# Attention scores of 64-deep heads as row-tiled groups of four matmuls, with new priority keys for the scheduler

## The chip, the cores and the metric

One Trainium2 chip, eight cores, two dies of four cores (0 to 3 and 4 to 7). Every core runs the same program on two of the sixteen sequences; no core talks to another. The metric is device time of the slowest core in microseconds (us); lower is better. Runs come in a fast state and a slow one (in the slow one a die, or both, shows a lower granted TensorE clock, down to 0.81 as the mean of a whole run); 12 of the 13 kernels run here had slow runs. All comparisons below are between fast runs or, where it is said, between cores of an undisturbed die.

## The reference, cut to what matters

A decoder layer: RMSNorm, one projection into a convolution part and an attention part, output projection, SwiGLU feed-forward (2816 wide), a gated per-layer embedding, final RMSNorm. The change is in the attention: 8 heads, each only 64 deep, sequence 4096, causal, with a decay per position.

```python
# logit[t, s] = q_t.k_s / sqrt(64) + c[t] - c[s],  c[t] = sum_{j<=t} log f[j]
s = jnp.einsum('bqhd,bkhd->bhqk', q_blk, kf)        # contraction over d = 64
s = s + c_q[..., :, None] - c_k[:, :, None, :]
s = jnp.where(k_pos[None, :] <= q_pos[:, None], s, -jnp.inf)
out = softmax(s) @ v
```

## The kernel before

The program is a list of operations, each with a priority key and a guessed duration; a list scheduler written in Python sets the order of each engine's queue when the kernel is built. The order is then fixed. 512 queries are one block; work of three blocks is mixed (attention of block n+1, feed-forward of block n, projections of block n+2), so that TensorE always has something to do. The keys say which of it goes first.

```python
KT = sb("KT", [128, 4, S], BF16)        # two heads stacked: head 2p in rows 0-63, head 2p+1 in 64-127
QT = sb("QT", [128, 8, T], BF16)        # per head; the other head's 64 rows are zero
qS = Pool("S", banks[0:3])              # 8 PSUM banks: scores,
qO = Pool("O", banks[3:5])              # attention output,
qD = Pool("Dn", banks[5:8])             # everything else
# ... [cut]
def fqk(e, st=st, hp=hp, kt=kt, c0=c0, dg=dg, h=h):          # one key tile of 128 keys
    ins = e.matmul(st.ap()[:, c0:T], lhsT=KT[:, hp, kt * 128:(kt + 1) * 128], rhs=QT[:, h, c0:T],
                   start=True, stop=not dg)
    if dg:                                                    # diagonal tile: decay, causal mask
        e.matmul(st.ap()[:, c0:T], lhsT=sel[:, h * 128:(h + 1) * 128], rhs=crow[:, c0:T],
                 start=False, stop=False)
        ins = e.matmul(st.ap()[:, c0:c0 + 128], lhsT=identb[:], rhs=maskb[:], start=False, stop=True)
    return ins
# ... then on ScalarE: P = exp(scores + bK); LOOK = 3 units later on TensorE: O += VA . P
```

Each score matmul contracts over 128 rows though a head has 64: the other 64 rows multiply zeros.

The softmax here doesn't subtract the row's maximum and nothing guards it: scores larger than these inputs give would overflow.

Of the kernel before, what the change touches and what calls it, by code (L numbers as in the profile page):

```python
# [7 lines left out]
F32 = mybir.dt.float32  # L8
# [11 lines left out]
SEQ_PER_CORE = 2  # L20
NEG = -30000.0
PAIRED = False

# [369 lines left out]
def build(nc, nblk=8, nseq=SEQ_PER_CORE):  # L393
# [22 lines left out]
    ones_d = dram("ones", [128, 128])  # L416
    maskb_d = dram("maskb", [128, 128])
    bdiag_d = dram("bdiag", [128, 128])
# [12 lines left out]
    onesf = sb("onesf", [128, 128], F32)  # L431
    maskb = sb("maskb_s", [128, 128], BF16)
    bdiag = sb("bdiag_s", [128, 128], BF16)
# [30 lines left out]
    B["sel"] = cdma("pool", sel[:], sel_d[:, :], 8 * K64, key=-1.19)  # L464
    B["maskb"] = cdma("pool", maskb[:], maskb_d[:, :], K64, key=-1.19)
    B["cw"] = cdma("sp", cw[:], cw_d[:, :], 8192, key=-1.0)
# [10 lines left out]

    KT = sb("KT", [128, 4, S], BF16)
    VA = sb("VA", [128, 32, 8, 65], BF16)
# [3 lines left out]
    ccar = sb("ccar", [128, 4, 2], F32)  # L483
    BKT = [[Buf() for _ in range(8)] for _ in range(4)]
    BVA = [Buf() for _ in range(32)]
# [28 lines left out]
    stat = sb("stat", [128, 64], F32)  # L514
    fst = sb("fst", [128, 8, 32], F32)
    Bfst = Buf()
# [5 lines left out]
    pXB = pool("xnbf", 2, [128, D], BF16)  # L522
    pP = pool("P", 5, [128, T], BF16)
    pCS = pool("cs", 1, [128, T], F32)
# [8 lines left out]
    banks = [es.enter_context(nc.psum_tensor(f"ps{i}", [128, 512], F32)) for i in range(8)]  # L533
    qS = Pool("S", banks[0:3])
    qO = Pool("O", banks[3:5])
    qD = Pool("Dn", banks[5:8])

    P.op("pool", lambda e: e.memset(VA[:, :, :, 64:65], 1.0), 1.0, -8.0, writes=BVA)
    P.op("pool", lambda e: e.memset(QT[:], 0.0), 2.0, -8.0, writes=BQT)
    P.op("pool", lambda e: e.memset(crow[:], 0.0), 0.6, -8.0, writes=[Bcrow])  # L540
# [121 lines left out]
    def qkv(m, kn, kk, kv, kq):  # L662
# [15 lines left out]
        for hp in range(4):  # L678
            t = Tile(qD)
            mm_group(t, fm_mats(wk[hp // 2], (hp % 2) * 128, w), kk + e_ * hp, xr + [wk[hp // 2]], gate=[BKT[hp][blk]])  # L680
            P.op("dve", lambda e, t=t, hp=hp: e.tensor_copy(out=KT[:, hp, q0:q0 + T], in_=t.ap()[:]),
                 0.69, kk + e_ * hp, reads=[t], writes=[BKT[hp][blk]])
        wv = [wload(g, kv) for g in plan["v"]]
# [33 lines left out]
        for hp in range(4):  # L717
            t = Tile(qD)
            mm_group(t, fm_mats(wq[hp // 2], (hp % 2) * 128, w), kq + e_ * hp, xr + [wq[hp // 2]], gate=[BQT[2 * hp], BQT[2 * hp + 1]])
            P.op("act", lambda e, t=t, hp=hp: e.activation(out=QT[0:64, 2 * hp, :], in_=t.ap()[0:64, :],  # L720
                                                           func=AF.Copy, scale=0.125),
                 0.6, kq + e_ * hp - 0.1, reads=[t], writes=[BQT[2 * hp]])
            P.op("dve", lambda e, t=t, hp=hp: e.tensor_scalar(out=QT[64:128, 2 * hp + 1, :], in0=t.ap()[64:128, :],
                                                              scalar1=0.125, scalar2=None, op0=ALU.mult),
                 0.69, kq + e_ * hp - 0.1, reads=[t], writes=[BQT[2 * hp + 1]])

# [54 lines left out]
    def decay(m, key):  # L781

        sq, blk = divmod(m, nblk)
        rel = fst[:, 6, :]
        P.op("dve", lambda e: e.tensor_copy(out=bK[:, 4 * blk:4 * blk + 4, :], in_=rel.rearrange("p (a b) -> p a b", a=4)),
             0.12, key, reads=[Brel], writes=[BbK])
        if blk:
            cb = carry[:, blk % 2, :].unsqueeze(1).to_broadcast([128, 4 * blk, 8])
            P.op("dve", lambda e: e.tensor_tensor(out=bK[:, 0:4 * blk, :], in0=cK[:, 0:4 * blk, :], in1=cb,
                                                  op=ALU.subtract),  # L790
                 0.35, key, reads=BcK[0:blk] + [Bcarry[blk % 2]], writes=[BbK])
        bx = Tile(qD)

        def ftr(e):
            ins = None
            for tt in range(4):
                ins = e.transpose(out=bx.ap()[0:8, tt * 128:(tt + 1) * 128], in_=fst[:, 6, 8 * tt:8 * tt + 8],
                                  identity=identf[:])
            return ins
        P.op("pe", ftr, 0.45, key, reads=[Brel, B["identf"]], writes=[bx], after=busy([Bcrow]))  # L800
        P.op("act", lambda e: e.activation(out=crow[0:8, :], in_=bx.ap()[0:8, :], func=AF.Copy, scale=-1.0),
             0.6, key - 0.1, reads=[bx], writes=[Bcrow])


    def attention(m, k0, k1):
        sq, blk = divmod(m, nblk)
        decay(m, k0 - 0.02)
        LOOK = 3
        units = []
# [30 lines left out]
        def post(h, o, key):  # L840
            q_ = osq[h % 2]
            P.op("act", lambda e: e.activation(out=q_[0:65, :], in_=o.ap()[0:65, :], func=AF.Square),
                 0.6, key - 0.1, reads=[o], writes=[Bosq[h % 2]])
            mt = Tile(qD)
            P.op("pe", lambda e: e.matmul(mt.ap()[:], lhsT=wn[:, :], rhs=q_[:, :], start=True, stop=True), MM,  # L845
                 key - 0.1, reads=[Bosq[h % 2], B["wn"]], writes=[mt])
            y0 = rsqrt_big(mt, 64, key - 0.1)
            if h % 2 == 0:
                dst = yTa[0:64, h // 2, :]
            else:  # L850
                dst = yTa[64:128, h // 2, :]
            P.op("dve", lambda e: e.scalar_tensor_tensor(out=dst, in0=o.ap()[0:64, :], scalar=gattn[:, h:h + 1],  # L852
                                                         in1=y0.ap()[0:64, :], op0=ALU.mult, op1=ALU.mult),
                 0.75, key - 0.1, reads=[o, y0, B["gattn"]], writes=[ByTa[h]])

        for i in range(N + LOOK):
            if i < N:
                h, kt, c0, dg, ui, nu = units[i]
                hp = h // 2
                if ui == 0 and blk:  # L860
# [7 lines left out]
                    P.op("act", lambda e, bt=bt, et=et: e.activation(out=et.ap()[0:65, :], in_=bt.ap()[0:65, :],  # L868
                                                                     func=AF.Exp), 0.6, K(i),
                         reads=[bt], writes=[et])  # L870
                st = Tile(qS)
                pt = Tile(pP)

                def fqk(e, st=st, hp=hp, kt=kt, c0=c0, dg=dg, h=h):
                    ins = e.matmul(st.ap()[:, c0:T], lhsT=KT[:, hp, kt * 128:(kt + 1) * 128], rhs=QT[:, h, c0:T],  # L875
                                   start=True, stop=not dg)
                    if dg:
                        e.matmul(st.ap()[:, c0:T], lhsT=sel[:, h * 128:(h + 1) * 128], rhs=crow[:, c0:T],  # L878
                                 start=False, stop=False)
                        ins = e.matmul(st.ap()[:, c0:c0 + 128], lhsT=identb[:], rhs=maskb[:], start=False, stop=True)  # L880
                    return ins
                w = (T - c0) / T
                rd = [BKT[hp][kt // 4], BQT[h]]
                if dg:
                    rd += [Bcrow, B["sel"], B["identb"], B["maskb"]]
                last_qk = P.op("pe", fqk, MM * w * (2 if dg else 1) + (0.06 if dg else 0.0), K(i), reads=rd,
                               writes=[st], after=[last_qk])
                P.op("act", lambda e, st=st, pt=pt, c0=c0, kt=kt, h=h: e.activation(  # L888
                    out=pt.ap()[:, c0:T], in_=st.ap()[:, c0:T], func=AF.Exp, bias=bK[:, kt, h:h + 1], scale=1.0),
                    0.17 + (T - c0) / 1200.0, K(i), reads=[st, BbK], writes=[pt])  # L890
                pend.append((h, kt, c0, dg, ui, nu, pt))
            if i >= LOOK:
# [219 lines left out]
    for n in range(-2, NB):  # L1112
# [7 lines left out]
        if 0 <= n + 1 < NB:  # L1120
# [3 lines left out]
            else:  # L1124
                conv(n + 1, b + 0.08, b + 0.5)
                attention(n + 1, b + 0.075, b + 0.95)
        if n >= 0:
            for tt in range(4):
                norm_tile((lambda tt=tt: hT[tt][:]), Bh[tt], tt, 1, 8, 4 + tt, b + 0.05)
            ffn(n, b + 0.07, b + 0.68)  # L1130
            for tt in range(4):
# [3 lines left out]
        if n + 2 < NB:  # L1135
# [4 lines left out]
            else:  # L1140
                qkv(n + 2, b + 0.5, b + 0.685, b + 0.8, b + 1.055)

# [9 lines left out]
def _host_consts():  # L1152
# [4 lines left out]
    c["ones"] = np.ones((128, 128), np.float32)  # L1157
    c["maskb"] = np.where(j[:, None] <= j[None, :], 0.0, NEG).astype(np.float32)
    c["bdiag"] = ((j[:, None] // 64) == (j[None, :] // 64)).astype(np.float32) / 64.0
# [5 lines left out]
    for h in range(8):  # L1165
        sel[h, h, :] = 1.0
    c["sel"] = sel.reshape(128, 1024)
    orow = np.zeros((128, 128), np.float32)
# [46 lines left out]
```

## Time and profile before

| what | value | read it as |
|---|---|---|
| time, fast runs | 4452.6 to 4455.2 us (6 of 16 runs) | the base of all that follows |
| time, slow runs | up to 5197 us | not compared |
| TensorE busy | 4310.9 us, 97% | the bound, but a modelled busy time: a 512-column matmul counts 380 ns on average, while starts are 216 ns apart (median) |
| TensorE waits that the profile lists | 123 us | 69 us of it in the first 150 and the last 200 us |
| ScalarE, VectorE, GpSimd busy | 51%, 59%, 4% | room |

TensorE waits for less than 3% of the time. Only less TensorE work, or work done two at a time, can help.

### The profile page before, as it was taken

Reading aid. Unit: us, or ns where it says so; the run is one execution under the profiler, and the core shown is the slowest. Engines: PE = TensorE matmul, PEld = TensorE weight load, DVE = VectorE, ACT = ScalarE, POOL = GpSimd, SP = SyncE. Lnnn points to the kernel's source line nnn. Section 1 sums busy time; section 2 is a strip of 40 time slices with the busy share of each in tenths; the row PEclk is TensorE's granted clock in tenths of the full one; section 3 lists DMA queues with packets and bytes.
Section 4 is the critical chain, followed back from the end, with each engine's and each line's share of the span. In section 5 each row is a group of like instructions: output and inputs, shape, how many; then the busy total and the mean of one; then the engine's idle time right before and its main releaser. Section 6 shows DMA issues by size and latency. Waiting matters only on the chain.

```text
span 4452.3 us, 75023 instructions; the slowest of 8 cores (4442.7 to 4452.3 us)
## 1 busy us (share of the span) xinstructions
PE 4310.9 (97%) x23984; PEld 2223.0 (50%) x23984; DVE 2644.5 (59%) x5380; ACT 2272.0 (51%) x4209; POOL 181.3 (4%) x405
## 2 busy tenths in 40 slices
PE   6899999999999999999999999999999999999987
PEld 3445454544545545445454545545454454554534
DVE  6667575665755645545676766757566464554444
ACT  3333354555646657567233444546455565666731
POOL 2110000000000000000000000000000000000000
PEclk9899999999999999999999999999999999999998
DMA  8796344343432433323444444434334343242232
GB/s 194 176 225 205 126 152 136 108 164 113 136 121 96 156 100 124 112 90 126 138 150 149 130 162 131 161 115 151 124 116 144 100 137 115 91 134 97 84 117 99
DMA packets 172924, 590.40 MB, mean 133 GB/s; under 512 B 19840, under 2 KB 28416, under 8 KB 172544
## 3 DMA queue, kind: packets, MB, share of 16 engines
q1 hardware_dynamic: 127952, 453.80, 30.8%
q0 software_dynamic: 44592, 131.79, 11.5%
q8 instruction: 207, 3.39, 0.3%
q14 instruction: 173, 1.42, 0.1%
HBM read 556.87 MB, written 61.87 MB: 139 GB/s over the span
## 4 chain that ended last, share of the span: by engine, by line
PE 91%; DVE 3%; issue 2%; DMA 2%; ACT 1%; POOL 0%; DVEq 0%; ACTq 0%; POOLq 0%; SPq 0%
PE ps L591 57%; PE ps L875 10%; PE ps L833 10%; PE ps L1079 5%; PE ps L709 2%; PE ps L639 2%; PE ps L878 1%; DMA xs<-x 1%; DVE ac L947 1%; DMA wslot<-wscr 1%; PE ps L1074 1%; PE ps L880 1%; PE ps L845 1%; PE ps L864 0%; DVE cu L937 0%
## 5 line engine op out<-in xcount | busy, mean ns | idle before, releaser
L888 ACT ACTIVATE P<-ps,bK 128x512 bf16<-128x512 f32 (+3 forms) x2304 | 1368.7, 650 | 811.8 <-PE ps L875 475.4
L591 PE MATMUL ps<-xnTd,wslot 128*128 128x512 bf16 x5792 | 1327.7, 380 | 9.2 <-DVE xnTd L644 3.4
L591 PEld LDWEIGHTS ps<-xnTd,wslot 128*128 128x128 bf16 x5792 | 562.0, 98 | 677.6 <-issue 33.6
L875 PE MATMUL ps<-QT,KT 128*128 128x512 bf16 (+3 forms) x2304 | 821.6, 362 | 13.5 <-ACT P L888 9.6
L833 PE MATMUL ps<-P,VA 128*65 128x512 bf16 (+3 forms) x2304 | 820.2, 363 | 5.6 <-DVE yTa L852 4.3
L591 PE MATMUL ps<-wslot,actT 128*128 128x512 bf16 x2816 | 652.5, 379 | 0.4 <-DVE h L976 0.4
L591 PE MATMUL ps<-xnTq,wslot 128*128 128x512 bf16 x2400 | 570.6, 382 | 13.3 <-DMA wslot<-wscr 7.8
L1021 DVE SCALAR_TENSOR_TENSOR tb<-th,ps 128x512 bf16<-128x512 f32 x352 | 241.2, 685 | 474.6 <-ACT th L1018 470.7
L1018 ACT ACTIVATE th<-ps 128x512 f32<-128x512 f32 x352 | 210.0, 596 | 484.5 <-PE ps L591 482.7
L591 PEld LDWEIGHTS ps<-wslot,actT 128*128 128x128 bf16 x2816 | 274.1, 98 | 318.6 <-issue 1.1
L976 DVE SCALAR_TENSOR_TENSOR h<-ps,h 128x512 f32<-128x512 f32 x256 | 176.2, 690 | 390.0 <-PE ps L591 388.2
L591 PEld LDWEIGHTS ps<-xnTq,wslot 128*128 128x128 bf16 x2400 | 231.2, 98 | 283.4 <-issue 33.7
L833 PEld LDWEIGHTS ps<-P,VA 128*65 128x65 bf16 x2304 | 257.1, 112 | 204.6 <-issue 11.8
L875 PEld LDWEIGHTS ps<-QT,KT 128*128 128x128 bf16 x2304 | 225.2, 98 | 261.8 <-issue 76.5
L622 ACT ACTIVATE xnbf<-h 128x1024 bf16<-128x1024 f32 x196 | 206.3, 1054 | 195.0 <-PE ps L639 76.7
L1025 DVE TENSOR_TENSOR actT<-tb,ps 128x512 bf16<-128x512 bf16 x352 | 241.1, 685 | 100.6 <-PE ps L591 96.7
L1079 PE MATMUL ps<-wslot,xnTd 128*128 128x256 bf16 x2048 | 247.9, 275 | 0.0
L1079 PEld LDWEIGHTS ps<-wslot,xnTd 128*128 128x128 bf16 x2048 | 201.8, 99 | 48.9 <-issue 1.0
L902 DVE TENSOR_TENSOR rs<-rs,ps 64x512 f32<-64x512 f32 (+1 forms) x192 | 130.1, 678 | 81.0 <-ACT rs L900 79.6
L644 DVE TENSOR_TENSOR xnTd<-ps,gpc_s 128x1024 bf16<-128x1024 bf16 x132 | 158.6, 1220 | 29.0 <-PE ps L639 27.1
L639 PE MATMUL ps<-identb,xnbf 128*128 128x128 bf16 x1536 | 119.2, 226 | 50.7 <-DVE stat L604 19.3
L1087 ACT ACTIVATE th<-ps 128x512 f32<-128x512 f32 x128 | 76.1, 594 | 166.7 <-PE ps L1079 132.4
(125 smaller groups left out, 4107.4 us busy)
## 6 DMA issues: line engine op xcount, KB each, us to landing
wslot<-wscr SPq DMA_DIRECT2D x795, 512.0 KB, 3.9
h<-x POOLq DMA_DIRECT2D x64, 512.0 KB, 6.3
y<-h POOLq DMA_DIRECT2D x64, 512.0 KB, 6.8
xs<-x POOLq DMA_DIRECT2D x60, 512.0 KB, 5.0
wslot<-wpack POOLq DMA_DIRECT2D x53, 512.0 KB, 14.7
wscr<-wslot SPq DMA_DIRECT2D x53, 512.0 KB, 10.9
wslot<-wscr SPq DMA_DIRECT2D x30, 256.0 KB, 2.7
pbf<-p POOLq DMA_DIRECT2D x16, 256.0 KB, 4.5
```

The costliest lines, as they stand in the source:

```text
L591: ins = e.matmul(out, lhsT=l, rhs=r, start=(i0 + i == 0), stop=(i0 + i == n - 1))
L622: P.op("act", lambda e: e.activation(out=xb.ap()[:], in_=src(), func=AF.Square, accum_out=stat[:, col:col + 1]), 1.25, key - 0.1, reads=[B ...
L639: ins = e.transpose(out=pv[:, kc * 128:(kc + 1) * 128], in_=xb.ap()[:, kc * 128:(kc + 1) * 128], identity=identb[:])
L644: P.op("dve", lambda e, pt=pt: e.tensor_tensor(out=xnT[which][:, :, tt * 128:(tt + 1) * 128], in0=pt.ap()[:].bitcast(BF16).rearrange("p (k ...
L833: P.op("pe", lambda e, o=o, kt=kt, h=h, pt=pt, c0=c0, first=first, last=last, ui=ui, dg=dg: e.matmul(o.ap()[0:65, c0:T], lhsT=VA[:, kt, h, ...
L875: ins = e.matmul(st.ap()[:, c0:T], lhsT=KT[:, hp, kt * 128:(kt + 1) * 128], rhs=QT[:, h, c0:T], start=True, stop=not dg)
L888: P.op("act", lambda e, st=st, pt=pt, c0=c0, kt=kt, h=h: e.activation(out=pt.ap()[:, c0:T], in_=st.ap()[:, c0:T], func=AF.Exp, bias=bK[:, ...
L976: P.op("dve", lambda e: e.scalar_tensor_tensor(out=hs, in0=t.ap()[:], scalar=scale, in1=hs, op0=ALU.mult, op1=ALU.add), 0.72, key - 0.05, ...
L1018: P.op("act", lambda e, tg=tg, th=th: e.activation(out=th.ap()[:], in_=tg.ap()[:], func=AF.Tanh, scale=0.5), 0.6, k - 0.1, reads=[tg], wri ...
L1021: P.op("dve", lambda e, tg=tg, th=th, tb=tb: e.scalar_tensor_tensor(out=tb.ap()[:], in0=th.ap()[:], scalar=1.0, in1=tg.ap()[:], op0=ALU.ad ...
L1025: P.op("dve", lambda e, tu=tu, tb=tb, j=j: e.tensor_tensor(out=actT[:, j, :], in0=tb.ap()[:], in1=tu.ap()[:], op=ALU.mult), 0.69, k - 0.1, ...
L1079: ins = e.matmul(tg.ap()[:, i * 256:(i + 1) * 256], lhsT=xnT[1][:, kc, ts], rhs=w8(wg[i])[:, kc, 0:256], start=False, stop=(kc == 7 and i ...
```

## The change

Intent: let matmuls of 64 rows run two at a time. Even key tiles of a head go to rows 0-63, odd ones to 64-127, the query of the head is copied to both halves, and four key tiles form a quad of four 64-row matmuls in alternating halves. The causal mask leaves TensorE: GpSimd zeroes the upper triangle of P. To find a fourth bank for scores, the other four are shared. Query and key evictions are split over ScalarE and VectorE. The keys of the scheduler are new.

```diff
-    KT = sb("KT", [128, 4, S], BF16)
+    KT = sb("KT", [128, 8, S // 2], BF16)
-    pP = pool("P", 5, [128, T], BF16)
+    pP = pool("P", 6, [128, T], BF16)
-    qS = Pool("S", banks[0:3])
-    qO = Pool("O", banks[3:5])
-    qD = Pool("Dn", banks[5:8])
+    qS = Pool("S", banks[0:4])
+    qO = Pool("Dn", banks[4:8])
+    qD = qO
 ... [cut: key and query evictions in four pieces, crow copied to rows 64-71, yTa product in two steps]
-        LOOK = 3
+        LOOK = 5
+                if ui % 4 == 0:
+                    quad = [Tile(qS) for _ in range(4)]
+                    def fqk(e, quad=quad, kt=kt, dg=dg, h=h):
+                        for dec in ((False, True) if dg else (False,)):
+                            for i in range(4):
+                                r = slice(64 * (i % 2), 64 * (i % 2) + 64)
+                                k_ = ((kt + i) // 2) * 128
+                                cc = 128 * i if dg else 0
+                                ins = e.matmul(quad[i].ap()[:, cc:T],
+                                               lhsT=sel[r, h * 128:(h + 1) * 128] if dec else KT[r, h, k_:k_ + 128],
+                                               rhs=crow[r, cc:T] if dec else QT[r, h, cc:T],
+                                               start=not dec, stop=dec or not dg)
+                        return ins
 ... [cut]
+                if dg:
+                    P.op("pool", lambda e, pt=pt, c0=c0: e.affine_select(
+                        out=pt.ap()[:, c0:c0 + 128], in_=pt.ap()[:, c0:c0 + 128], pattern=[[1, 128]],
+                        compare_op=ALU.is_ge, fill=zero_reg(e), base=0, channel_multiplier=-1),
+                        0.35, K(i), writes=[pt])
 ... [cut]
-                conv(n + 1, b + 0.08, b + 0.5)
-                attention(n + 1, b + 0.075, b + 0.95)
+                conv(n + 1, b + 0.08, b + 0.556)
+                attention(n + 1, b + 0.05, b + 0.815)
-            ffn(n, b + 0.07, b + 0.68)
+            ffn(n, b + 0.138, b + 0.695)
-                qkv(n + 2, b + 0.5, b + 0.685, b + 0.8, b + 1.055)
+                qkv(n + 2, b + 0.504, b + 0.685, b + 0.788, b + 1.017)
```

More of the change, by code (lines that the diff above doesn't have):

```diff
@@ L20 @@
 SEQ_PER_CORE = 2
-NEG = -30000.0
-PAIRED = False
 SEED_SCALE = -0.5 * float(np.log(2.0)) / 2.0 ** 23
@@ L416, in build @@
     ones_d = dram("ones", [128, 128])
-    maskb_d = dram("maskb", [128, 128])
     bdiag_d = dram("bdiag", [128, 128])
@@ L431, in build @@
     onesf = sb("onesf", [128, 128], F32)
-    maskb = sb("maskb_s", [128, 128], BF16)
     bdiag = sb("bdiag_s", [128, 128], BF16)
@@ L464, in build @@
     B["sel"] = cdma("pool", sel[:], sel_d[:, :], 8 * K64, key=-1.19)
-    B["maskb"] = cdma("pool", maskb[:], maskb_d[:, :], K64, key=-1.19)
     B["cw"] = cdma("sp", cw[:], cw_d[:, :], 8192, key=-1.0)
@@ L483, in build @@
     ccar = sb("ccar", [128, 4, 2], F32)
-    BKT = [[Buf() for _ in range(8)] for _ in range(4)]
+    BKT = [[Buf() for _ in range(8)] for _ in range(8)]
     BVA = [Buf() for _ in range(32)]
@@ L514, in build @@
     stat = sb("stat", [128, 64], F32)
-    fst = sb("fst", [128, 8, 32], F32)
+    fst = sb("fst", [128, 7, 32], F32)
     Bfst = Buf()
@@ L533, in build @@
     banks = [es.enter_context(nc.psum_tensor(f"ps{i}", [128, 512], F32)) for i in range(8)]
-    qS = Pool("S", banks[0:3])
-    qO = Pool("O", banks[3:5])
-    qD = Pool("Dn", banks[5:8])
+    qS = Pool("S", banks[0:4])
+    qO = Pool("Dn", banks[4:8])
+    qD = qO
     P.op("pool", lambda e: e.memset(VA[:, :, :, 64:65], 1.0), 1.0, -8.0, writes=BVA)
-    P.op("pool", lambda e: e.memset(QT[:], 0.0), 2.0, -8.0, writes=BQT)
     P.op("pool", lambda e: e.memset(crow[:], 0.0), 0.6, -8.0, writes=[Bcrow])
@@ L679, in qkv @@
             t = Tile(qD)
-            mm_group(t, fm_mats(wk[hp // 2], (hp % 2) * 128, w), kk + e_ * hp, xr + [wk[hp // 2]], gate=[BKT[hp][blk]])
-            P.op("dve", lambda e, t=t, hp=hp: e.tensor_copy(out=KT[:, hp, q0:q0 + T], in_=t.ap()[:]),
-                 0.69, kk + e_ * hp, reads=[t], writes=[BKT[hp][blk]])
+            mm_group(t, fm_mats(wk[hp // 2], (hp % 2) * 128, w), kk + e_ * hp, xr + [wk[hp // 2]], gate=[BKT[2 * hp][blk], BKT[2 * hp + 1][blk]])
+            for i in range(2):
+                for par in range(2):
+                    src = (lambda t=t, i=i, par=par: t.ap()[64 * i:64 * i + 64, :].rearrange(
+                        "p (a b c) -> p a b c", a=2, b=2)[:, :, par, :])
+                    dst = KT[64 * par:64 * par + 64, 2 * hp + i, q0 // 2:q0 // 2 + 256].rearrange("p (a c) -> p a c", a=2)
+                    if i == 0:
+                        P.op("act", lambda e, src=src, dst=dst: e.activation(out=dst, in_=src(), func=AF.Copy),
+                             0.39, kk + e_ * hp - 0.1, reads=[t], writes=[BKT[2 * hp + i][blk]])
+                    else:
+                        P.op("dve", lambda e, src=src, dst=dst: e.tensor_copy(out=dst, in_=src()),
+                             0.42, kk + e_ * hp - 0.1, reads=[t], writes=[BKT[2 * hp + i][blk]])
         wv = [wload(g, kv) for g in plan["v"]]
@@ L719, in qkv @@
             mm_group(t, fm_mats(wq[hp // 2], (hp % 2) * 128, w), kq + e_ * hp, xr + [wq[hp // 2]], gate=[BQT[2 * hp], BQT[2 * hp + 1]])
-            P.op("act", lambda e, t=t, hp=hp: e.activation(out=QT[0:64, 2 * hp, :], in_=t.ap()[0:64, :],
-                                                           func=AF.Copy, scale=0.125),
-                 0.6, kq + e_ * hp - 0.1, reads=[t], writes=[BQT[2 * hp]])
-            P.op("dve", lambda e, t=t, hp=hp: e.tensor_scalar(out=QT[64:128, 2 * hp + 1, :], in0=t.ap()[64:128, :],
-                                                              scalar1=0.125, scalar2=None, op0=ALU.mult),
-                 0.69, kq + e_ * hp - 0.1, reads=[t], writes=[BQT[2 * hp + 1]])
+            for i in range(2):
+                for half in range(2):
+                    src = (lambda t=t, i=i: t.ap()[64 * i:64 * i + 64, :])
+                    dst = QT[64 * half:64 * half + 64, 2 * hp + i, :]
+                    if i == 0:
+                        P.op("act", lambda e, src=src, dst=dst: e.activation(out=dst, in_=src(), func=AF.Copy, scale=0.125),
+                             0.6, kq + e_ * hp - 0.1, reads=[t], writes=[BQT[2 * hp + i]])
+                    else:
+                        P.op("dve", lambda e, src=src, dst=dst: e.tensor_scalar(
+                            out=dst, in0=src(), scalar1=0.125, scalar2=None, op0=ALU.mult),
+                            0.69, kq + e_ * hp - 0.1, reads=[t], writes=[BQT[2 * hp + i]])
     def gate_post(m, zt, key):
@@ L800, in decay, with zero_reg @@
         P.op("pe", ftr, 0.45, key, reads=[Brel, B["identf"]], writes=[bx], after=busy([Bcrow]))
-        P.op("act", lambda e: e.activation(out=crow[0:8, :], in_=bx.ap()[0:8, :], func=AF.Copy, scale=-1.0),
-             0.6, key - 0.1, reads=[bx], writes=[Bcrow])
+        for r in (0, 64):
+            P.op("act", lambda e, r=r: e.activation(out=crow[r:r + 8, :], in_=bx.ap()[0:8, :], func=AF.Copy, scale=-1.0),
+                 0.6, key - 0.1, reads=[bx], writes=[Bcrow])
+    zreg = []
+    def zero_reg(e):
+        if not zreg:
+            zreg.append(e.to_reg(0.0))
+        return zreg[0]
     def attention(m, k0, k1):
@@ L843, in post @@
                  0.6, key - 0.1, reads=[o], writes=[Bosq[h % 2]])
+            dst = yTa[0:64, h // 2, :] if h % 2 == 0 else yTa[64:128, h // 2, :]
+            P.op("dve", lambda e: e.tensor_scalar(out=dst, in0=o.ap()[0:64, :], scalar1=gattn[:, h:h + 1], scalar2=None,
+                                                  op0=ALU.mult), 0.69, key - 0.1, reads=[o, Bosq[h % 2], B["gattn"]], writes=[ByTa[h]])
             mt = Tile(qD)
@@ L851, in post @@
                 dst = yTa[64:128, h // 2, :]
-            P.op("dve", lambda e: e.scalar_tensor_tensor(out=dst, in0=o.ap()[0:64, :], scalar=gattn[:, h:h + 1],
-                                                         in1=y0.ap()[0:64, :], op0=ALU.mult, op1=ALU.mult),
-                 0.75, key - 0.1, reads=[o, y0, B["gattn"]], writes=[ByTa[h]])
+            P.op("dve", lambda e: e.tensor_tensor(out=dst, in0=dst, in1=y0.ap()[0:64, :], op=ALU.mult),
+                 0.69, key - 0.1, reads=[y0], writes=[ByTa[h]])
         for i in range(N + LOOK):
@@ L868, in attention @@
                     P.op("act", lambda e, bt=bt, et=et: e.activation(out=et.ap()[0:65, :], in_=bt.ap()[0:65, :],
-                                                                     func=AF.Exp), 0.6, K(i),
+                                                                     func=AF.Exp, scale=0.5), 0.6, K(i),
                          reads=[bt], writes=[et])
-                st = Tile(qS)
                 pt = Tile(pP)
-                def fqk(e, st=st, hp=hp, kt=kt, c0=c0, dg=dg, h=h):
-                    ins = e.matmul(st.ap()[:, c0:T], lhsT=KT[:, hp, kt * 128:(kt + 1) * 128], rhs=QT[:, h, c0:T],
-                                   start=True, stop=not dg)
-                    if dg:
-                        e.matmul(st.ap()[:, c0:T], lhsT=sel[:, h * 128:(h + 1) * 128], rhs=crow[:, c0:T],
-                                 start=False, stop=False)
-                        ins = e.matmul(st.ap()[:, c0:c0 + 128], lhsT=identb[:], rhs=maskb[:], start=False, stop=True)
-                    return ins
@@ L882, in attention @@
-                w = (T - c0) / T
-                rd = [BKT[hp][kt // 4], BQT[h]]
-                if dg:
-                    rd += [Bcrow, B["sel"], B["identb"], B["maskb"]]
-                last_qk = P.op("pe", fqk, MM * w * (2 if dg else 1) + (0.06 if dg else 0.0), K(i), reads=rd,
-                               writes=[st], after=[last_qk])
+                if ui % 4 == 0:
[11 more added lines that the diff above has]
+                        return ins
+                    rd = [BKT[h][kt // 4], BQT[h]]
+                    if dg:
+                        rd += [Bcrow, B["sel"]]
+                    last_qk = P.op("pe", fqk, (3 * MM if dg else 2 * MM) + 0.2, K(i), reads=rd, writes=quad,
+                                   after=[last_qk])
@@ L888, in attention @@
+                st = quad[ui % 4]
                 P.op("act", lambda e, st=st, pt=pt, c0=c0, kt=kt, h=h: e.activation(
@@ L1157, in _host_consts @@
     c["ones"] = np.ones((128, 128), np.float32)
-    c["maskb"] = np.where(j[:, None] <= j[None, :], 0.0, NEG).astype(np.float32)
     c["bdiag"] = ((j[:, None] // 64) == (j[None, :] // 64)).astype(np.float32) / 64.0
@@ L1166, in _host_consts @@
         sel[h, h, :] = 1.0
+        sel[64 + h, h, :] = 1.0
     c["sel"] = sel.reshape(128, 1024)
```

## The prediction

> **What bounds the kernel now.** I read the cores first (is the run disturbed?), then the busy shares, the chain of work that ended last, the matmul groups by shape, and last a few microseconds of the time line, because a busy TensorE is not yet a full one.
>
> ```profile
> core 7: 4452.3 us, clock 0.989
> die 0 (median of its cores): 4448.6 us, clock 0.990
> die 1 (median of its cores): 4447.5 us, clock 0.991
> ```
>
> All cores end within 10 us of each other at full clock: no core and no die is special, and I can reason on one of them.
>
> ```profile
> PE 4310.9 (97%) x23984; PEld 2223.0 (50%) x23984; DVE 2644.5 (59%) x5380; ACT 2272.0 (51%) x4209; POOL 181.3 (4%) x405
> ...
> PE 91%; DVE 3%; issue 2%; DMA 2%; ACT 1%; POOL 0%; DVEq 0%; ACTq 0%; POOLq 0%; SPq 0%
> ```
>
> TensorE is 97% busy and makes up 91% of the chain; VectorE and ScalarE have 40 to 50% to spare, GpSimd nearly all. So time follows TensorE's stream, unless a change makes it wait.
>
> ```profile
> L833 PE MATMUL ps<-P,VA 128*65 128x512 bf16 x1920 | 728.4, 380 | 5.6 <-DVE yTa L852 4.3 <-DVE ps L828 1.1
> L875 PE MATMUL ps<-QT,KT 128*128 128x512 bf16 x1920 | 717.7, 380 | 12.4 <-ACT P L888 8.5 <-ACT stat L606 2.9
> ...
> L880 PE MATMUL ps<-maskb_s,identb 128*128 128x128 bf16 x512 | 112.5, 220 | 0.0
> ```
>
> The score matmuls (QT,KT) are the object of the change: 1920 of full width and 384 narrower ones, with only 12.4 us of idle time ahead of them. The 380 ns is a duration with its pipeline; what one costs in a stream is the distance between starts:
>
> ```profile
> 2008.56 0.38 PE L875 MATMUL ps<-QT,KT 128*128 128x512 bf16 x1
> 2008.77 0.38 PE L833 MATMUL ps<-P,VA 128*65 128x512 bf16 x1
> 2008.99 0.38 PE L875 MATMUL ps<-QT,KT 128*128 128x512 bf16 x1
> 2009.20 0.38 PE L833 MATMUL ps<-P,VA 128*65 128x512 bf16 x1
> ```
>
> Starts are 0.2155 us apart for 512 columns: that, not 0.380, is the price. 0.165 us of each duration is pipeline that the next matmul hides. With 0.2155 us per 512 columns (in proportion for narrower ones, plus 2 ns each) all matmuls of the program sum to 4246 us; the other 206 us are the start, the tail and small gaps.
>
> [...]
>
> **The change part by part.** Now each score matmul contracts over 128 rows of which 64 are the other head's keys against zeros in QT. The change stores keys so that even key tiles of a head lie in rows 0-63 and odd ones in rows 64-127, and copies each head's query to both halves. Four key tiles form a quad: four 64-row matmuls, alternating halves, into four banks of PSUM.
>
> 1. *Full quads.* 1792 unmasked score matmuls make 448 quads. Four at 0.2155 = 0.862 us become two pairs, 0.431 us. Saved 448 x 0.431 = 193 us.
> 2. *Diagonal quads.* 16 blocks x 8 heads = 128. Score and decay matmuls of 512, 384, 256 and 128 columns, 2560 columns, cost 1.085 us; paired (512 beside 384, 256 beside 128, twice) 1536 columns, 0.65 us. Saved 128 x 0.435 = 56 us.
> 3. *The mask matmul goes.* 512 of 128 columns at 0.0556 us: 28 us. Its work moves to GpSimd, one select of 128x128 per diagonal tile.
> 4. *Mode changes.* Every quad is entered from and left to 128-row work: 576 x 2 changes. In the instruction order of the built program nearly every quad stands alone between other matmuls. [...] The kernel's own scheduler charges a quad with 0.2 us beyond its pairs. I take 0.2 us for both changes, an estimate: 576 x 0.2 = 115 us lost.
> 5. *Other engines.* ScalarE: 128 key copies at about 0.38, 64 more query copies at 0.587 and 16 crow copies at 0.58 add about 95 us to 2272. VectorE: keys +10, queries 64 x 0.694 = 44, the yTa product split in two (128 x 2 x 0.69 less 128 x 0.742 = 82) add about 136 to 2645. GpSimd: 512 selects at about 0.35 (its 4096-element memset took 3.87 us) 180 us. All beside TensorE, none a bound: 56%, 65% and 9% of 4300.
> 6. *New waits.* The four score banks are now one unit: a quad starts only when all four exponentials of the last are done. Back to back, three exponentials took 1.84 us, 0.58 apart, so four take 2.4 us and a quad's round trip about 3.2 us with its matmuls, pipeline and signals. Adding up, in the instruction order, the TensorE work from each quad to the next against this round trip plus the other ScalarE work between, TensorE has less in only 14 of 575 places, 15 us in all, at the start and in the last block. GpSimd's queue is in order and holds loads of h that wait for a store to land (113 us idle before them, up to 8.6 at once); selects behind them can hold up a head. I add 20 us for both.
>
> Sum: 193 + 56 + 28 - 115 - 20 = 142 us. 4453 - 142 is 4311; [...] I say 4300.
>
> **The rivals.**
> (a) *Perfect pairs, cheap switches.* If a switch costs only a weight load's few tens of ns (0.1 us per quad): 58 instead of 115, about 4245. For: the array is entered within 40 ns of a weight load after idle in the trace.[...]
> (b) [...] If both changes cost the whole 0.165 us plus some 0.04 of weight load, 0.41 us per quad, 236 us: 4430, the same within 2%.[...]
> (c) *No pairing on the chip.* Two tiles that run one after the other leave only the mask: 28 - 115 - 20, some 4560.[...]
> (d) *ScalarE or PSUM becomes the bound.* In the deepest block of a sequence 64 quads need about 215 us of round trips, in a block where TensorE has some 270 to 300 us of work; close, but under. Merging O and Dn into four shared banks could make the feed-forward wait for a bank; before, TensorE waited on evictions for under 10 us. If both bite, 4350 to 4400.
>
> **Range and chances.** The switch cost dominates: 0.1 us per quad more or less is 58 us. From 0.1 with few waits (4235) to 0.3 with double the waits (4388): range 4225 to 4400. Under 4365 (2% faster) needs a quad below about 0.3 us of switching: 0.80. Within 2%: 0.17 (rival b, or d with a costly switch). Slower by over 2%: 0.03 (rival c).
>
> **What would show it.** Pairs: two score matmuls of a quad start within some ns, and the next two about 0.22 us later; if all four are 0.22 apart, rival c. Switch: the distance from the start of the second pair to the start of the next 128-row matmul, less 0.2155, and the same going in; together 0.2 us. Waits: idle time before the score matmuls released by exponentials, before the P,VA matmuls released by GpSimd, together near 20 us. ScalarE near 2370 and VectorE near 2780 us busy. What would make it wrong: switches far from 0.1 us each, a falling granted clock[...], or GpSimd selects several times longer than 0.35 us.

## The result, and the profile after

The changed kernel takes 4298 to 4305 us in six of its seven fast runs (the seventh, 4340, had a lower clock on one die, 0.974 to 0.981 against 0.987 to 0.989 on the other; the median of all 11 runs is 4304.86), against 4453 us: some 150 us less. The ratio of the fast runs is 0.967, with a 95% interval of 0.964 to 0.970. (Ratios are the mean time of one kernel's fast runs over that of the other's of the same rounds, so not quite the ratio of the medians quoted.)

The cores of the profiled run, the busy shares and the chain of work that ended last, after the change:

```profile
core 5: 4297.3 us, clock 0.986
...
die 0 (median of its cores): 4290.8 us, clock 0.987
die 1 (median of its cores): 4292.5 us, clock 0.988
```

```profile
PE 4154.0 (97%) x23472; PEld 2002.4 (47%) x23472; DVE 2778.9 (65%) x5636; ACT 2352.5 (55%) x4417; POOL 357.1 (8%) x915
...
PE 88%; DMA 5%; issue 2%; DVE 2%; ACT 1%; POOL 0%; another core or an unknown queue 0%; DVEq 0%; POOLq 0%; ACTq 0%; SPq 0%
```

TensorE is as busy as before over a shorter span: still the bound. The 512 matmuls that are gone are the masks. The groups of matmuls by shape show where the time came from (line numbers have moved: L901 is the score line, L850 the P,VA line, L916 the select):

```profile
L850 PE MATMUL ps<-P,VA 128*65 128x512 bf16 x1920 | 615.8, 385 | 9.9 <-POOL P L916 2.8 <-ACT P L912 2.7 <-ACT stat L600 2.0
L901 PE MATMUL ps<-QT,KT 64*128 64x512 bf16 x1920 | 322.0, 383 | 9.1 <-ACT P L912 5.6 <-ACT QT L729 3.0 <-ACT crow L811 0.5
```

The mean duration of a score matmul has not changed (383 ns after, 380 before), but the union of their busy time has fallen from 717.7 to 322.0 us: they lie on top of each other. The time line of TensorE around one full quad (start, duration) shows both the gain and its price:

```profile
2577.26 0.38 PE L988 MATMUL ps<-epsr,onesrow_s 128*128 128x512 bf16 x1
2577.48 0.38 PE L850 MATMUL ps<-P,VA 128*65 128x512 bf16 x1
2577.79 0.61 PE L901 MATMUL ps<-QT,KT 64*128 64x512 bf16 x4
2578.32 0.41 PE L850 MATMUL ps<-P,VA 128*65 128x512 bf16 x1
```

Four score matmuls end 0.61 us after the first began, and the next one starts 0.53 us after. But the matmul ahead of the quad holds TensorE for 0.31 us in place of 0.22, and the quad for 0.53 in place of 0.43. Over all 448 full quads of this core's trace the starts within a quad lie at 0, 3, 226 and 230 ns (medians), the entry costs 96 ns beyond the price of the matmul ahead, and its 10th percentile is 95: it is a constant, not a wait that sometimes occurs.

### The profile page after: what moved, and what is told of

It reads as the page before. It is cut to its first block, busy times and chain, and to the rows that moved or that the text cites. A ratio compares the mean times of both kernels' runs of the same rounds, so it can differ in the third digit from the quotient of the medians.

```text
span 4297.3 us, 74891 instructions; the slowest of 8 cores (4285.3 to 4297.3 us)
## 1 busy us (share of the span) xinstructions
PE 4154.0 (97%) x23472; PEld 2002.4 (47%) x23472; DVE 2778.9 (65%) x5636; ACT 2352.5 (55%) x4417; POOL 357.1 (8%) x915
## 4 chain that ended last, share of the span: by engine, by line
PE 88%; DMA 5%; issue 2%; DVE 2%; ACT 1%; POOL 0%; another core or an unknown queue 0%; DVEq 0%; POOLq 0%; ACTq 0%; SPq 0%
PE ps L585 57%; PE ps L850 11%; PE ps L901 7%; PE ps L1108 5%; PE ps L713 2%; DMA wslot<-wpack 2%; PE ps L633 2%; DMA wscr<-wslot 1%; DMA xs<-x 1%; DMA y<-h 1%; PE ps L1103 1%; PE ps L865 1%; PE ps L883 1%; DMA h<-x 1%; ACT P L912 0%
## 5 line engine op out<-in xcount | busy, mean ns | idle before, releaser
L585 PE MATMUL ps<-xnTd,wslot 128*128 128x512 bf16 x5792 | 1354.1, 381 | 6.9 <-DVE xnTd L638 3.5
L850 PE MATMUL ps<-P,VA 128*65 128x512 bf16 (+3 forms) x2304 | 677.5, 368 | 13.3 <-POOL P L916 6.1
L585 PE MATMUL ps<-wslot,actT 128*128 128x512 bf16 x2816 | 662.8, 379 | 2.0 <-DMA wslot<-wpack 2.0
L850 PEld LDWEIGHTS ps<-P,VA 128*65 128x65 bf16 x2304 | 239.9, 111 | 342.2 <-issue 190.1
L1047 ACT ACTIVATE th<-ps 128x512 f32<-128x512 f32 x352 | 209.8, 596 | 297.9 <-PE ps L585 295.4
L901 PE MATMUL ps<-QT,KT 64*128 64x512 bf16 (+3 forms) x2304 | 336.4, 365 | 9.1 <-ACT P L912 5.6
L916 POOL TENSOR_SCALAR_AFFINE_SELECT P<-P 128x128 bf16<-128x128 bf16 x512 | 180.0, 359 | 1824.2 <-ACT P L912 1702.8
L901 PEld LDWEIGHTS ps<-QT,KT 64*128 64x128 bf16 x2304 | 66.5, 94 | 228.9 <-issue 225.7
L931 DVE TENSOR_TENSOR rs<-rs,ps 128x512 f32<-128x512 f32 (+1 forms) x192 | 130.1, 678 | 66.4 <-ACT rs L929 65.7
```

Of the source, the lines that this page charges most:

```text
L585: ins = e.matmul(out, lhsT=l, rhs=r, start=(i0 + i == 0), stop=(i0 + i == n - 1))
L850: P.op("pe", lambda e, o=o, kt=kt, h=h, pt=pt, c0=c0, first=first, last=last, ui=ui, dg=dg: e.matmul(o.ap()[0:65, c0:T], lhsT=VA[:, kt, h, ...
L901: ins = e.matmul(quad[i].ap()[:, cc:T], lhsT=sel[r, h * 128:(h + 1) * 128] if dec else KT[r, h, k_:k_ + 128], rhs=crow[r, cc:T] if dec els ...
L916: P.op("pool", lambda e, pt=pt, c0=c0: e.affine_select(out=pt.ap()[:, c0:c0 + 128], in_=pt.ap()[:, c0:c0 + 128], pattern=[[1, 128]], compa ...
L1047: P.op("act", lambda e, tg=tg, th=th: e.activation(out=th.ap()[:], in_=tg.ap()[:], func=AF.Tanh, scale=0.5), 0.6, k - 0.1, reads=[tg], wri ...
```

## The experiments

Eleven kernels ran, in twelve runs (one kernel twice) and three groups, each group on one chip. The kernel before ran in each group too, at 4451 to 4456 us in its fast runs, so the chips can be compared. Slow runs are left out. The first four take the gain apart.

**1. No concurrency: all four matmuls in one half.** The order, the 64-row mode and the mode changes stay; odd key tiles are wrong, so the result is wrong on purpose.

```diff
-                                r = slice(64 * (i % 2), 64 * (i % 2) + 64)
+                                r = slice(0, 64)
```

> The changed kernel with all four matmuls of a quad in rows 0 to 63 (odd key tiles wrong, so a wrong result on purpose); the order of instructions, the 64-row mode and the number of mode changes stay. Theory (the pairs run at the same time and that carries the gain): starts inside a quad go from 3, 226, 229 ns to about 216, 432, 648 ns, a full quad costs 0.42 us more, a diagonal one 0.43, so 448 x 0.42 + 128 x 0.43 = 243 us more than the changed kernel: about 4545 us. Rival (the gain is the dropped mask matmul and the newly tuned order, the pairs are hidden behind waits): under 50 us more, below 4350.

Measured: 4537.2 and 4537.4 us in the fast runs, 237 us more than the changed kernel. The same quad on its time line:

```profile
2709.65 0.38 PE L850 MATMUL ps<-P,VA 128*65 128x512 bf16 x1
2709.97 1.03 PE L901 MATMUL ps<-QT,KT 64*128 64x512 bf16 x4
2710.93 0.41 PE L850 MATMUL ps<-P,VA 128*65 128x512 bf16 x1
```

0.96 us from the quad to the next matmul, in place of 0.53; the entry, 0.32, is what it was. The theory holds: pairs run at the same time, and that is worth 237 us.

**2. No mode change: all 128 rows.** Again wrong on purpose (each score is the sum of two key tiles), with the same order and the same semaphore waits.

```diff
-                                r = slice(64 * (i % 2), 64 * (i % 2) + 64)
+                                r = slice(0, 128)
```

> The changed kernel with each matmul of a quad over all 128 rows (sums of two key tiles, a wrong result on purpose): the order and waits of the changed kernel, no pairs and no mode change. Theory (the 96 ns ahead of a quad and the 95 to 120 ns behind it are the change of tiling mode): both go to near 0, so it is 576 x 0.21 = about 120 us shorter than the one with four serial matmuls in 64-row mode: about 4425 us. Rival (the gaps are the quad's own semaphore waits and not the mode): the gaps stay, and it is within 20 us of that one, about 4545.

Measured: 4417.8 us in its profiled fast run, 119 us less than run 1. (The other run counted as fast took 4462.6 us, with one die at a clock of 0.976 to 0.982; its other die took at most 4415.5.) The time line at the same place:

```profile
2643.70 0.38 PE L850 MATMUL ps<-P,VA 128*65 128x512 bf16 x1
2643.91 1.03 PE L901 MATMUL ps<-QT,KT 128*128 128x512 bf16 x4
2644.78 0.38 PE L850 MATMUL ps<-P,VA 128*65 128x512 bf16 x1
```

The entry is 0.21 us, the bare price of the matmul ahead, and the exit 0.87, four bare prices. So the gaps belong to the change between 128-row and 64-row matmuls (the change of mode) and not to the quad's waits. 119 us over 576 quads are 0.21 us for going in and out once.

What the change of mode holds up can be seen on the time line of the weight loads (engine PEld) at the same two places. In run 2 the quad's first weights start to load at 2643.70, as the matmul ahead begins; in the changed kernel they start at 2577.78, 0.30 us after the matmul ahead began and just before the quad itself. Over all 576 quads the first load starts 214 ns (median) ahead of the first matmul in run 2, as it does before the 1920 full score matmuls of the kernel before, and within 10 ns of it at 556 of them in the changed kernel: at those 556 the weights were not loaded ahead over the change of mode. What holds them there is not shown.

**3. Groups of two.** Correct result; the number of groups nearly doubles.

```diff
-                if ui % 4 == 0:
+                if ui % 2 == 0:
-                    quad = [Tile(qS) for _ in range(4)]
+                    quad = [Tile(qS) for _ in range(2)]
 ... [cut: loops over 2, diagonal pairs start at column c0, guessed duration of a group]
```

> The changed kernel with groups of two score matmuls in place of four (correct result): twice as many mode changes, half as many banks held per group. Theory: 576 more groups at 0.21 to 0.23 us each make 120 to 130 us more, about 4425 to 4435 us, and the cost of one group stays 96 ns in and some 95 ns plus 25 out. Rival (the round trip of four exponentials on a single-buffered set of banks is what costs): two groups in flight hide it and the time falls below 4300.

Measured: 4416.5 to 4418.0 us in three of its four runs (4443.3 in the other, with one die at 0.979 to 0.984), 117 us more. A few groups met others back to back, so its trace has 1128 entries where the quads had 576: 117 us over 552 added entries are 0.21 us again. Two groups in flight did not help.

**4. The mask alone.** The kernel before, with its mask matmul replaced by the GpSimd select.

```diff
-                        e.matmul(st.ap()[:, c0:T], lhsT=sel[...], rhs=crow[:, c0:T], start=False, stop=False)
-                        ins = e.matmul(st.ap()[:, c0:c0 + 128], lhsT=identb[:], rhs=maskb[:], start=False, stop=True)
+                        ins = e.matmul(st.ap()[:, c0:T], lhsT=sel[...], rhs=crow[:, c0:T], start=False, stop=True)
+                if dg: P.op("pool", ... e.affine_select(...) ..., 0.35, K(i), writes=[pt])
```

> The kernel before with only the causal mask moved from a TensorE matmul to a GpSimd select (correct result). Theory: 512 matmuls of 0.056 us go, 28 us less, some 5 to 10 us come back as waits for GpSimd with only three units of look-ahead: 4430 to 4435 us. Rival (the select on the way from the exponential to the P,VA matmul holds TensorE up): no gain or slower, 4450 to 4480.

Measured: 4447.2 to 4448.4 us, 6 us less: neither the 4430 to 4435 of the theory nor the 4450 or more of the rival. That sent me to the look-ahead (by how many key tiles the scores run ahead of the P,VA product) in run 8.

The second group looks at what made the rest of the program tolerate quads.

**5. The old keys.**

```diff
-                attention(n + 1, b + 0.05, b + 0.815)
+                attention(n + 1, b + 0.075, b + 0.95)
-            ffn(n, b + 0.138, b + 0.695)
+            ffn(n, b + 0.07, b + 0.68)
 ... [cut: convolution and projections likewise]
```

> The changed kernel with the priority keys of the kernel before (convolution, attention, feed-forward and projections), so another order of the same instructions (correct result). Theory (TensorE has work in nearly any order, so the keys are worth little): within 20 us of the changed kernel, 4290 to 4325 us. Rival (the keys were tuned to quads, and part of the gain is theirs): 4340 us or more, with TensorE waiting more before the P,VA or score matmuls.

Measured: 4430.0 to 4432.8 us (ratio to the kernel before 0.9955). My theory fell at once: of the 150 us only some 20 are left. The TensorE waits of this run that have to do with exponentials, then those of the changed kernel (waiting line, what it waited for, us in total, times, longest; rows that belong to the program's start are left out):

```profile
PE ps L901 <- ACT P L912: 33.8, 47, 3.0
PE ps L850 <- ACT P L912: 17.0, 47, 0.9
...
PE ps L850 <- POOL P L916: 10.5, 14, 2.2
```

```profile
PE ps L850 <- POOL P L916: 6.1, 8, 1.6
PE ps L901 <- ACT P L912: 5.6, 9, 1.7
```

Quads wait for exponentials. The time line of the run with old keys, at the end of a block's attention, shows how:

```profile
2077.46 0.61 PE L901 MATMUL ps<-QT,KT 64*128 64x512 bf16 x4
2078.00 0.40 PE L850 MATMUL ps<-P,VA 128*65 128x512 bf16 x1
2079.00 0.38 PE L850 MATMUL ps<-P,VA 128*65 128x512 bf16 x1 [0.60 <-ACT P L912]
2079.58 0.38 PE L850 MATMUL ps<-P,VA 128*65 128x512 bf16 x1 [0.20 <-ACT P L912]
2080.16 0.38 PE L850 MATMUL ps<-P,VA 128*65 128x512 bf16 x1 [0.20 <-ACT P L912]
```

After the quad TensorE has only P,VA matmuls left, and these come at the pace of the exponentials, 0.58 us apart. The old keys end the feed-forward at 0.68 of a block and attention at 0.95, so the last part of attention runs with little else to put between. Summed over all rows, the listed waits are 192 us here and 126 us in the changed kernel: 66 of the 132 us. The granted clock is also lower (0.976 of 4430 us against 0.986 of 4297 us on the two slowest cores), which is 106 against 60 us of clock not granted; with the medians of the dies (0.981 against 0.987) it is some 25 to 30 us more and not 46. In steps of 20 us from 1900 to 2140 of the run with old keys the clock is lower in and just after the stretches where TensorE is least busy: 0.83 from 2040 (15.71 us busy), 0.86 from 2080 (15.52), 0.93 from 2100 (17.71) and 0.87 from 2120 (19.61); it is 1.00 in the other eight, with 18.70 us busy or more. The same 20 us on the slowest core with the old keys and in the changed kernel (columns as in run 8 below; 15.52 and 20.00 are TensorE's busy time, 0.86 and 1.00 the clock):

```profile
2080.00:2100.00 20.00, 15.52 (x77) 6.36 (x78) 9.59 (x15) 11.99 (x24) 6.13 (x11) 0.86 0.17 56
```

```profile
2080.00:2100.00 20.00, 20.00 (x94) 9.12 (x93) 10.25 (x18) 4.18 (x8) 1.11 (x3) 1.00 0.59 187
```

If the lower clock comes with the waits, as in these stretches, a wait cost twice here; no run separates the two. I can account for some 95 to 112 us that way, if the two parts don't overlap; the rest is not explained. All four keys were changed together, so which of them matters is not shown either.

**6. The shared banks parted.**

```diff
-    qO = Pool("Dn", banks[4:8])
-    qD = qO
+    qO = Pool("O", banks[4:6])
+    qD = Pool("Dn", banks[6:8])
```

> The changed kernel with its four shared PSUM banks parted into two for the attention output and two for all else (correct result). Theory (sharing is what keeps the fourth score bank from costing anything): the feed-forward then works with two banks instead of three or so, TensorE waits on evictions by VectorE and ScalarE, and the time rises by 40 us or more, above 4340. Rival (two are enough, as attention fills the waits): under 15 us more, below 4320.

Measured: 4557.8 us in its profiled run, the only fast one of five, 258 us more, slower than the kernel before. In the other runs the cores of the undisturbed die took 4540 to 4561 us.

```profile
PE ps L585 <- DVE h L1002: 38.5, 6, 10.7
PE ps L585 <- ACT QT L729: 18.3, 18, 3.9
PE ps L1103 <- ACT th L1116: 18.3, 37, 0.8
```

TensorE now waits for evictions in the projections and the gate of the embedding. The theory's sign was right, its size far too small: with these keys, parting the four banks two and two loses more than the whole gain. Another parting, or keys tuned for parted banks, was not tried.

**7. The old look-ahead.**

```diff
-        LOOK = 5
+        LOOK = 3
```

> The changed kernel with the look-ahead of the kernel before, three units in place of five (correct result). With three, the first P,VA matmul of a quad is asked for before the next quad. Theory (the wait for an exponential and its select needs the longer look-ahead, but TensorE has other work): 5 to 20 us more, 4305 to 4325 us. Rival (the look-ahead carries the hiding of exponential and select): over 40 us more, with waits of P,VA for exponentials and selects.

Measured: 4324.4 and 4324.7 us, 25 us more; between my two figures, nearer the theory.

**8. The mask alone, with look-ahead five and six P buffers.**

```diff
 (run 4) [cut: the unused mask tile and its load go]
-        LOOK = 3
+        LOOK = 5
-    pP = pool("P", 5, [128, T], BF16)
+    pP = pool("P", 6, [128, T], BF16)
```

> The kernel before with the mask moved to GpSimd, as in an earlier run that gained 6 us of the 28 us of matmuls removed, and now with five units of look-ahead and six P buffers as in the changed kernel (correct result). Theory (three units are too few once a select stands between exponential and P,VA): 4425 to 4433 us, 20 us or more under the kernel before. Rival (the missing 20 us are not the look-ahead's): 4440 us or more.

Measured: 4424.3 us in its only fast run (the profiled one was slow), so I repeated it in the third group:

> The run of the kernel before with the mask on GpSimd and five units of look-ahead, once more, as only one of its five runs was in the fast state. Theory: fast runs again near 4424 us, so the whole 28 us of the mask matmuls is gained with the longer look-ahead. Rival (that one run was a stray): 4440 us or more.

4424.8 to 4428.8 us, ratio 0.9941: some 26 us less than the kernel before, the 28 us of the masks nearly whole. So the 20 us missing in run 4 were lost to the short look-ahead or to the smaller number of P buffers; which of the two is not told apart. Run 7, which moved the look-ahead alone in the changed kernel, cost 25 us and speaks for the look-ahead.

The profiled slow run of this kernel shows what the slow state is (columns: stretch, busy time and count of TensorE, weight loads, VectorE, ScalarE, GpSimd, then granted clock, DMA share, GB/s):

```profile
1000.00:1100.00 100.00, 99.86 (x557) 56.72 (x556) 65.44 (x154) 53.16 (x101) 6.83 (x18) 0.81 0.37 122
3000.00:3100.00 100.00, 97.18 (x645) 57.25 (x644) 80.54 (x193) 55.94 (x110) 9.69 (x23) 1.00 0.46 151
```

For a part of this run the clock is 0.81, later it is full again. In other slow runs it lasts: in one of the slow runs of run 1 the four cores of die 1 average 0.808 to 0.812 over the whole run, and die 0 has 0.986 or more.

The third group asks what the keys really do.

**9. The new keys in the kernel before.**

> The kernel before with nothing but the changed kernel's priority keys (correct result). The old keys had cost the changed kernel 130 us. Theory (the keys matter only with quads; the kernel before waits on TensorE for no more than 123 us, most of it at the start and the end of the program): within 15 us of the kernel before, 4440 to 4470 us. Rival (the new keys are simply better, and part of the change's gain has nothing to do with row tiles): 4420 us or less.

The edit is run 5's, the other way round, in the kernel before. Measured: 4422.8 us in the best run and 4449.7 in the profiled one; ratio 0.996 with an interval of 0.991 to 1.001, so the same within 2% by the verdict, and not clear of no change at all. In the profiled run die 0 was disturbed (clocks down to 0.981, spans up to 4448 us); the cores of the undisturbed die:

```profile
core 4: 4413.8 us, clock 0.991
core 5: 4419.4 us, clock 0.989
core 6: 4416.7 us, clock 0.991
core 7: 4421.9 us, clock 0.990
```

In the kernel before these four cores took 4443 to 4452 us, and in the three slow runs of this kernel the undisturbed die took at most 4421.6 to 4422.5. So the new keys are worth about 30 us to the kernel before, too: neither my theory (within 15) nor quite the rival.

**10. Quads over 128 rows, with the old keys.** Run 2 with the edit of run 5.

> The run with quads over all 128 rows (no pairs, no mode change, a wrong result on purpose), with the priority keys of the kernel before. Theory (what the old keys hurt is the quad as a unit: four banks held together, so each next quad waits for four exponentials, and the old keys leave the end of attention without other work to put between): the penalty of the old keys stays about as large as with pairs, 80 to 140 us over 4418, so 4500 to 4560 us. Rival (what they hurt is that paired matmuls leave TensorE too little work beside ScalarE): with the slower quads the penalty falls under 40 us, below 4460.

Measured: 4533.6 to 4538.0 us, ratio to the kernel before 1.018: 118 us more than run 2. TensorE waits 38.2 us for exponentials before score matmuls here, 6.0 us in run 2. Slower score matmuls do not save the old keys.

**11. Groups of two, with the old keys.** Run 3 with the edit of run 5.

> The run with groups of two score matmuls (row tiles, correct result), with the priority keys of the kernel before. Two groups can be in flight here, as the four banks are taken two at a time. Theory (the unit of four banks is what needs other work between): the penalty of the old keys is less than half of the 130 us that quads paid, 4430 to 4480 us. Rival (the faster score matmuls are the cause, however grouped): 100 us or more, above 4515.

Measured: 4453.5 to 4455.9 us, 37 us more than run 3. With two banks per group the penalty falls from 132 to 37 us, about what the kernel before paid. So it is the quad as a unit of four banks that needs the new keys, and not the faster matmuls.

No run beat the changed kernel. What is left to take is the 119 us of mode changes; larger groups would need more score banks, which no run tried.

## Why the prediction was right or wrong

The number held for the fast state: 4300 predicted, 4298 to 4305 measured in undisturbed runs. Two steps of the prediction failed all the same.

- *The base of the sum, 4453 us.* It was read off one profile in which all cores had a clock of 0.99, and the range was laid about it without a word on the slow state; a falling clock stood only among the things that would make it wrong. In the fast runs with clocks on record no core averaged less than 0.974. In slow runs it was 0.81 over long stretches, and 0.808 to 0.812 on one die over a whole run (run 8). Ten of the 16 runs of the kernel before were slow, and the median of all 16 is 4554 us; scaled with the ratio of 0.967 that makes 4404 us, just outside the range. A base and a range have to name the state that they are for.
- *Step 6, new waits: 20 us lost.* The waits that the profile lists before TensorE went from 123.3 to 125.6 us: 2 us. The two kinds that the prediction told the reader to look for came to 11.7 us (5.6 before score matmuls for exponentials, 6.1 before P,VA for selects), and 9.6 us of the first kind were there before. The step took the order with the new keys as given and so missed what keeps the waits small: with the old keys the list grows to 192 us and the time by 132 us (run 5). That a load of h can hold up a select behind it does show in the trace of the changed kernel: a load waited 7.05 us for a store to land, and the select after it began at 2981.02, 0.01 us after the load's issue, though the last exponential had ended at 2979.78; a P,VA matmul then waited 0.42 us for a select.

The steps one by one:

- *Bound.* Right. TensorE is the bound before and after, and ScalarE (2352 us, predicted near 2370) and VectorE (2779, predicted near 2780) stayed beside it. The 4246 us of matmuls don't follow from the rule written beside them, which gives 4203: in the trace the next matmul starts 25 ns after an 8-column bf16 one and 107 to 112 ns after an fp32 one (medians by shape, 8 to 128 columns). With the distances measured for each shape I get 4249. The price of 512 columns holds: over all of them in the kernel before, the next matmul starts 216 ns later (median; 215 at the 10th percentile).
- *Steps 1 and 2, the pairs: 193 + 56 = 249 us.* All 23984 matmuls of the kernel before use 128 rows, so that two of 64 rows run at the same time was the author's assumption. Right: 237 us between run 1 and the changed kernel. Second tiles start 3 ns after the first, second pairs at 226 ns; about 220 was named.
- *Step 3, the mask: 28 us.* Right in size, 26 us in run 8, but only with the longer look-ahead and the sixth P buffer; alone it brought 6 us. The step did not name that condition.
- *Step 4, the mode changes: 0.2 us a quad, 115 us.* No trace of the kernel before shows a change of mode; the 0.2 was the author's estimate, the figure that the kernel's own scheduler uses. Right: 119 us, 0.21 us, by two routes (runs 1 and 2, run 3). Rivals a (0.1) and b (0.41) are both out, and rival c (no pairing) with run 1.
- *The last correction, from 4311 to 4300.* Wrong. It took part of a mode change to hide behind the quad's wait, the author's assumption. The entry is 95 to 97 ns at the 10th, 50th and 90th percentile; next to nothing hides. The sum was rounded down for a reason that isn't there.
- *Step 5, other engines.* Right; the 512 selects took 180.0 us, 180 was said (mean 359 ns, median 292, the longest 3.3 us).
- *Step 6 as a term of the sum.* It held the wrong things. Run 2 has no pairs, no mode changes and no mask; against 4453 it took off 35 us. The masks explain 26, so quads, banks and keys together brought some 9 us where the prediction put a loss of 20. The term that it missed is the keys: in the kernel before they bring about 30 us (run 9). If the parts simply add, which no run shows, quads and banks then cost about 20 us, what was written, and the keys paid it back.
- *Rival d.* It has the shared banks only as a risk; parted two and two they lose 258 us. Its 64 round trips of 3.2 us are 205 us, not 215.

So the mechanism and its two large terms were sized well, and that the sum came out so close is luck: the prediction has some 29 us of gain too much (12 in the pairs, 2 in the mask, 4 in the mode changes, 11 in the rounding) and 29 too little in step 6. Open are the split of look-ahead and P buffers in run 8, some 20 to 40 us of run 5, which of the four keys matters, and why the slow state comes when it does.

## What to carry to other kernels

Two row tiles of 64 really did run at the same time here (the second starts 3 ns after the first), and the price was 0.21 us for each trip into the mode and back. So count the trips first: a quad of 512-column matmuls saved 0.43 us and paid half of it back. Then look for what the group holds as one unit, here four banks until four exponentials are done, and give the engine other work for just that time; with keys that did not, the changed kernel kept only some 20 of its 150 us.
